# Another hand-written order of the steps in the two local-attention stages of a four-layer decoder trunk

## The chip, the core and the metric

The kernel runs on one core of one Trainium2 chip. Its time is that of one launch on the device in microseconds (us). Five engines with an instruction queue each share the work: TensorE (PE, matmuls and transposes; PEld are its weight loads), VectorE (DVE), ScalarE (ACT), GpSimd (POOL) and SyncE (SP, which here issues the loads of weights). An engine takes its instructions in the order in which they stand in its queue; between engines semaphores order the work.

## The reference, cut to what matters

A trunk of four layers over 256 rows of 1024 numbers in float32. Each layer has a token mixer, a cross-attention and a gated MLP, each followed by a LayerNorm. The mixers of layers 0 and 3 are the local attention that the change touches:

```
qkv = x @ w_qkv                                   # 16 query heads, 4 key/value groups, 64 wide
q, k = apply_rope(q), apply_rope(k)
scores = einsum('bnqhgd,bnkhd->bnhgqk', qb, kb) * 64 ** -0.5      # 128-row blocks, own and previous block
scores = where(valid, scores, -1e30)
probs = softmax(concatenate([scores, sink], -1))[..., :-1]        # a learned sink per head
out = einsum('bnhgqk,bnkhd->bnqhgd', probs, vb).reshape(...) @ w_o
```

## The kernel before, in words

Weights come from memory in pieces of up to 1 MB (`raw`). ACT casts each piece to a high part (`whi`, line 287) and DVE subtracts to get the low part (`wlo`, line 288), four pairs of 512 columns for a piece; a large product is then three matmuls (high by high, high by low, low by high). Four split pieces can be held; a slot comes free when the last matmul on its piece is done. A piece is split by ticks that the large matmuls give, so casts and subtractions stand between the other instructions of ACT and DVE.

A local-attention stage (function `swa`) first projects keys and values. Then `play` walks through a string of tokens, `SWA_SEQ`, a letter for the step and a number for the key group (0 to 3; a group has four query heads):

- Q: query projection of a group, 48 large matmuls (line 352) into one bank of PSUM.
- R: rotary on DVE, lines 685 to 689: three products from PSUM and a sum into `ropet`.
- K: keys to the layout with the head dimension on partitions: 8 transposes (line 359), two copies on ACT into `kT` (line 773).
- U: the same for the group's queries: 4 transposes, one copy on ACT into `qT` (line 699).
- S: scores: 8 small matmuls for the first row block and 8 for the second as the trace counts them, into four banks; DVE adds the mask and takes the maximum of each head (line 722, 8 instructions), three small ones (lines 725 to 727), and ACT takes 9 exponentials (lines 728 and 731).
- N: DVE sums, takes the reciprocal and multiplies (lines 737 to 740).
- T: 12 transposes of the probabilities into three banks, three copies on ACT into `pt` (line 750).
- P: probabilities by values, then a cast on ACT (`oh`, line 370) and a subtraction on DVE (`ol`, line 371).
- C: a chunk of the output projection, 12 matmuls of 512 columns. W loads the square-root table on ACT (line 408), G loads the LayerNorm's vectors.

The four tiles of the last two groups go through `op.finish`, where the LayerNorm begins. PSUM has eight banks, and from the first C on the output holds four of them.

```
def q_turn(g):
    ...
    A.copy(out=qT, in_=tp)
...
def scores(g):
    ...
    last[0] = A.activation(out=pr[:, hd], in_=pr[:, hd], func=AF.Exp, ...)
...
play(SWA_SEQ, {"Q": q_proj, "K": k_turn, "R": q_rope, "U": q_turn, "S": scores, "N": normalize, "T": turn, "P": pv, ...})
```

The tokens set in which order the steps are handed over. A scheduler then places each engine's instructions by its own estimate of when they are ready, so the queue of an engine can hold the steps in another order than the string; that order is fixed when the kernel is built. The two stages run from the same string, but what surrounds them differs, and so can their queues.

Of the kernel before, what the change touches and what calls it, by code (L numbers as in the profile page):

```python
# [32 lines left out]
PHASES = [("mem", 0)]  # L33
for _i in range(DEPTH):
    PHASES += [(("swa", "rglru", "mla")[_i % 3], _i), ("cross", _i), ("ffn", _i)]
SWA_SEQ = ("Q0 R0 Q1 R1 U0 Q3 K0 U1 R3 S0 S1 N0 Q2 T0 U3 P0 R2 U2 S3 N1 N3 T1 S2 C0 P1 N2 C1 W0 T2 T3 C2 P2 P3 "
           "C3 G0")
RG_SEQ = ("a2 t0 b2 V1 a3 V0 V2 b3 A1 V3 g0 h0 A2 g2 A0 g1 A3 R3 R2 R0 R1 h1 Z0 E0 g3 E1 h3 Y0 C0 G0 h2 E2 E3 "
          "C1 Y1 C2 Y2 Y3 W0 C3")
# [16 lines left out]
def _plan():  # L56
# [8 lines left out]
    def cols_piece(key, name, idx, cols):  # L65
        n = (cols.stop - cols.start) if isinstance(cols, slice) else len(cols)
        add(key, KC * n, lambda I: _b_piece(I[name] if idx is None else I[name][idx], cols))

    def halves(tag, name, idx, cols):
        n = (cols.stop - cols.start) if isinstance(cols, slice) else len(cols)  # L70
        for h in range(2):
            add((tag, h), 4 * n, lambda I, h=h: _b_piece(
                (I[name] if idx is None else I[name][idx])[512 * h:512 * h + 512], cols))

    def order(seq, pieces):
        for tok in seq.split():
            for toks, fn in pieces:
                if tok in toks.split():
                    pieces.remove((toks, fn))
                    fn()  # L80
                    break
# [7 lines left out]
    def outs(tag, name, idx):  # L89
        return [(f"C{2 * c} C{2 * c + 1}", lambda c=c: out_piece(tag, name, idx, c)) for c in range(2)]  # L90
# [5 lines left out]
    def piece_swa(i):  # L96
        j = i // 3
        halves(("kv", i), "a_w_qkv", j, slice(1024, 1536))
        order(SWA_SEQ, [(f"Q{g}", lambda g=g: cols_piece(("q", i, g), "a_w_qkv", j, slice(256 * g, 256 * g + 256)))
                        for g in range(A_G)] + outs(("mo", i), "a_w_o", j))  # L100
# [234 lines left out]
def trunk(ctx, tc, x_in, xT_in, memT_in, w, par, con, sinks, ln_g, ln_b, out):  # L335
# [70 lines left out]
    def want_sqrt(last):  # L406
        with tc.issue_after(ins_of(last)):
            A.activation(out=epsl[:, 2:3], in_=epsl[:, 0:1], func=AF.Sqrt)
# [202 lines left out]
    def play(seq, table):  # L611
        for tok in seq.split():
            table[tok[0]](int(tok[1]))
# [46 lines left out]
    def swa(mx, i, rest):  # L660
# [119 lines left out]
        def gb(_):  # L780
            norm[0] = Norm(op.y, mx, "p1", 2, i, 0)

        play(SWA_SEQ, {"Q": q_proj, "K": k_turn, "R": q_rope, "U": q_turn, "S": scores, "N": normalize, "T": turn, "P": pv,
                       "C": chunk, "G": gb, "W": lambda _: want_sqrt(last[0])})
# [493 lines left out]
```

## Time and profile before

| | us |
|---|---|
| median of 3 runs | 1384.0 (1383.43 to 1384.91) |
| the profiled execution | 1384.68 |
| its span, first to last instruction | 1382.7 |
| PE busy | 1363.8 (99%) |
| DVE busy | 1084.8 (78%) |
| ACT busy | 881.1 (64%) |
| first local attention, from its first query projection to the last C ahead of the finish | 65.7 to 119.85 |
| second local attention, end of the same stretch | 1113.56 |

A matmul's record runs until its results are out, so records overlap and PE looks busy through short waits. Waits are better seen at the weight loads (PEld): each load is followed by its matmul, and an idle time in front of a load is a wait. The granted clock of TensorE stands in the tables by stretch.

### The profile page before, as it was taken

To read this page: it belongs to the slowest core of one execution; us is meant where nothing else is said; L and a number is where in the kernel's file an instruction comes from. 1 tells how busy PE (TensorE), PEld (TensorE's weight loads), DVE (VectorE), ACT (ScalarE), POOL (GpSimd) and SP (SyncE) were. 2 spreads that over 40 slices of the span, in tenths; PEclk is the share of its full clock that TensorE was granted. 3 is DMA by queue.
4 is the path that set the end of the run, shared out by engine and by line. 5 is a ranking of instruction groups with operands and counts; after the bars stand their busy time and mean duration, and the time that the engine had idled before them with its cause. 6 is when DMAs were issued, how large, how long until landed. Compare 5 with 4: busy or idle time off the path is not lost.

```text
span 1382.7 us, 23749 instructions
## 1 busy us (share of the span) xinstructions
PE 1363.8 (99%) x9110; PEld 1232.0 (89%) x9110; DVE 1084.8 (78%) x2392; ACT 881.1 (64%) x1892; POOL 13.0 (1%) x28
## 2 busy tenths in 40 slices
PE   8999999999999999999999999999999999999997
PEld 8887989999898898999988898999998789899996
DVE  6887869777788878877778687977779867797775
ACT  6666747555579666655557664855565856675553
POOL 0000000000000000000000000000000000000000
PEclk9999999999999999999999999999999999999999
DMA  8733536555535554655526442555554326455550
GB/s 319 273 137 122 203 104 246 205 189 183 183 123 184 199 196 168 225 187 183 179 103 236 153 176 99 214 214 185 192 195 148 135 94 228 166 214 183 185 182 31
DMA packets 39393, 246.78 MB, mean 178 GB/s; under 512 B 4336, under 2 KB 6640, under 8 KB 12400
## 3 DMA queue, kind: packets, MB, share of 16 engines
q1 hardware_dynamic: 35824, 232.69, 46.3%
q0 software_dynamic: 3456, 12.58, 2.7%
q8 instruction: 71, 1.16, 0.3%
q14 instruction: 42, 0.34, 0.1%
HBM read 244.21 MB, written 1.05 MB: 177 GB/s over the span
## 4 chain that ended last, share of the span: by engine, by line
PE 92%; ACT 3%; DVE 3%; issue 0%; DMA 0%; SPq 0%; DVEq 0%; ACTq 0%
PE ps L352 89%; PE ps L359 3%; ACT p L731 2%; DVE p L722 1%; DVE wlo L288 1%; DMA raw<-in_w_dram 0%; DVE tt L834 0%; ACT whi L287 0%; DVE x L478 0%; DVE x L480 0%; DVE x L454 0%; DVE tt L832 0%; ACT oh L370 0%; ACT tt L861 0%; DVE ropet L689 0%
## 5 line engine op out<-in xcount | busy, mean ns | idle before, releaser
L288 DVE TENSOR_TENSOR wlo<-raw,whi 128x512 fp32r<-128x512 f32 (+1 forms) x869 | 559.1, 683 | 149.5 <-ACT whi L287 143.0
L287 ACT CAST whi<-raw 128x512 fp32r<-128x512 f32 (+1 forms) x869 | 485.9, 619 | 174.6 <-PE ps L352 150.2
L352 PE MATMUL ps<-xh,whi 128*128 128x256 f32 x1504 | 421.2, 280 | 0.0
L352 PE MATMUL ps<-xh,wlo 128*128 128x256 f32 x1504 | 420.1, 279 | 0.0
L352 PE MATMUL ps<-xl,whi 128*128 128x256 f32 x1504 | 419.8, 279 | 0.0
L352 PEld LDWEIGHTS ps<-xl,whi 128*128 128x128 f32 x1504 | 282.7, 188 | 1.9
L352 PEld LDWEIGHTS ps<-xh,whi 128*128 128x128 f32 x1504 | 282.7, 188 | 1.8
L352 PEld LDWEIGHTS ps<-xh,wlo 128*128 128x128 f32 x1504 | 282.6, 188 | 0.0
L1151 DVE SCALAR_TENSOR_TENSOR cv<-ps,part,cv 128x255 f32<-128x255 f32 (+1 forms) x352 | 166.3, 477 | 3.8 <-ACT cv L1149 1.4
L352 PE MATMUL ps<-whi,xh 128*128 128x512 f32 (+3 forms) x336 | 118.4, 353 | 0.4 <-ACT xh L370 0.2
L352 PE MATMUL ps<-wlo,gh 128*128 128x512 f32 x352 | 116.0, 396 | 0.0
L352 PE MATMUL ps<-whi,gh 128*128 128x512 f32 x352 | 115.9, 396 | 0.0
L352 PE MATMUL ps<-wlo,xh 128*128 128x512 f32 (+3 forms) x336 | 115.7, 345 | 0.0
L352 PE MATMUL ps<-whi,gl 128*128 128x512 f32 x352 | 115.1, 393 | 0.0
L1149 ACT ACTIVATE cv<-ps,part 128x256 f32<-128x256 f32 x176 | 98.3, 563 | 16.9 <-DVE cv L1151 5.5
L370 ACT CAST gh<-cv 128x256 fp32r<-128x256 f32 x88 | 35.7, 406 | 107.2 <-DVE cv L1166 107.0
L352 PE MATMUL ps<-whi,oh 128*128 128x512 f32 x256 | 92.9, 403 | 3.4 <-ACT oh L370 3.4
L352 PE MATMUL ps<-whi,xl 128*128 128x512 f32 (+3 forms) x336 | 92.6, 347 | 0.0
L352 PE MATMUL ps<-wlo,oh 128*128 128x512 f32 x256 | 90.8, 394 | 0.0
L352 PE MATMUL ps<-whi,ol 128*128 128x512 f32 x256 | 90.6, 395 | 0.0
L352 PEld LDWEIGHTS ps<-whi,gl 128*128 128x128 f32 x352 | 66.3, 188 | 15.8
L352 PEld LDWEIGHTS ps<-wlo,gh 128*128 128x128 f32 x352 | 66.4, 189 | 15.3
(227 smaller groups left out, 1842.1 us busy)
## 6 DMA issues: line engine op xcount, KB each, us to landing
raw<-in_w_dram SPq DMA_DIRECT2D x210, 1024.0 KB, 4.8
lng<-in_ln_g_dram POOLq DMA_DIRECT2D x12, 512.0 KB, 4.5
lnb<-in_ln_b_dram POOLq DMA_DIRECT2D x12, 512.0 KB, 6.2
raw<-in_w_dram SPq DMA_DIRECT2D x5, 768.0 KB, 4.7
raw<-in_w_dram SPq DMA_DIRECT2D x5, 256.0 KB, 6.1
raw<-in_w_dram SPq DMA_DIRECT2D x2, 640.0 KB, 3.7
xf<-in_xT_dram SPq DMA_DIRECT2D x1, 1024.0 KB, 8.6
x<-in_x_dram SPq DMA_DIRECT2D x1, 1024.0 KB, 13.2
```

The lines of the kernel that those rows point to most:

```text
L287: self.nc.scalar.copy(out=hi[:, c], in_=raw[:, c])
L288: self.nc.vector.tensor_tensor(out=lo[:, c], in0=raw[:, c], in1=hi[:, c].bitcast(F32), op=ALU.subtract)
L352: T.matmul(o, lhsT=l, rhs=r, start=st, stop=sp, **kw)
L359: T.transpose(o, i, ident)
L370: a = A.copy(out=hi, in_=src)
L722: V.tensor_tensor_reduce(out=pr[:, hd], in0=sc[e][:, c], in1=mk, scale=1.0, scalar=-3e38, op0=ALU.add, op1=ALU.max, accum_out=m[:, tb, hd: ...
L731: last[0] = A.activation(out=pr[:, hd], in_=pr[:, hd], func=AF.Exp, scale=A_D ** -0.5, bias=nm[:, b, hd:hd + 1], accum_out=sm[:, b, hd:hd ...
L1149: A.activation(out=dst, in_=src, func=AF.Identity, scale=wc[:, taps - 1:taps], bias=bias)
L1151: V.scalar_tensor_tensor(out=dst[:, d:], in0=src[:, :S - d], scalar=wc[:, taps - 1 - d:taps - d], in1=dst[:, d:], op0=ALU.mult, op1=ALU.add)
```

## The change

Only the string of tokens is changed. What each step computes is the same.

```
-SWA_SEQ = ("Q0 R0 Q1 R1 U0 Q3 K0 U1 R3 S0 S1 N0 Q2 T0 U3 P0 R2 U2 S3 N1 N3 T1 S2 C0 P1 N2 C1 W0 T2 T3 C2 P2 P3 "
-           "C3 G0")
+SWA_SEQ = ("Q0 R0 Q1 R1 K0 U0 U1 S0 S1 Q2 N0 R2 Q3 N1 R3 T0 U2 P0 T1 S2 P1 U3 S3 C0 N2 C1 W0 N3 C2 T2 T3 P2 P3 "
+           "C3 G0")
```

The keys' transposes and the scores of groups 0 and 1 now stand right behind Q0 and Q1, and the projections Q2 and Q3 follow them without a step between. Group 2 goes ahead of group 3 in everything that follows, U3 stands behind P1, and N3 behind C1. The pieces of weights for Q2 and Q3 change places with them.

ACT's queue of the first stage, before, from the copies of T0 on (p_1121 and p_1186 are the scores of groups 3 and 2):

```order
L750 COPY pt<-ps 128x512 x3
L699 COPY qT<-ps 128x512
L287 CAST whi<-raw 128x512 x2
L370 CAST oh<-ps 128x2x2x128
L699 COPY qT<-ps 128x512
L287 CAST whi<-raw 128x512 x2
L750 COPY pt<-ps 128x512 x3
L731 ACTIVATE p_1121,sm<-p_1121,nm 128x128
L728 ACTIVATE es<-es 128x8
L731 ACTIVATE p_1121,sm<-p_1121,nm 128x128 x3
L731 ACTIVATE p_1122,sm<-p_1122,nm 128x256 x4
```

The same place in the changed kernel, from the copies of T1 on (p_1137 and p_1138 are the scores of group 2, p_1193 and p_1194 those of group 3):

```order
L750 COPY pt<-ps 128x512 x3
L287 CAST whi<-raw 128x512
L370 CAST oh<-ps 128x2x2x128
L728 ACTIVATE es<-es 128x8
L731 ACTIVATE p_1137,sm<-p_1137,nm 128x128 x4
L731 ACTIVATE p_1138,sm<-p_1138,nm 128x256 x4
L699 COPY qT<-ps 128x512
L731 ACTIVATE p_1193,sm<-p_1193,nm 128x128
L728 ACTIVATE es<-es 128x8
L731 ACTIVATE p_1193,sm<-p_1193,nm 128x128 x3
L731 ACTIVATE p_1194,sm<-p_1194,nm 128x256 x4
L408 ACT_TABLE_LOAD
```

Before, both late copies into `qT` stand ahead of all exponentials of groups 3 and 2. In the changed kernel the copy for group 3 stands behind the nine exponentials of group 2.

The second stage of the changed kernel, the same place on ACT (p_12021 and p_12022 belong to group 2):

```order
L750 COPY pt<-ps 128x512 x3
L287 CAST whi<-raw 128x512
L370 CAST oh<-ps 128x2x2x128
L699 COPY qT<-ps 128x512
L731 ACTIVATE p_12021,sm<-p_12021,nm 128x128
L728 ACTIVATE es<-es 128x8
L731 ACTIVATE p_12021,sm<-p_12021,nm 128x128 x3
L731 ACTIVATE p_12022,sm<-p_12022,nm 128x256 x4
```

Here the copy for group 3 stands ahead of the exponentials of group 2.

PE's queue of the first stage in the changed kernel, behind Q3 (T0, U2, P0, T1, S2, P1, U3, S3, and the first row of C0):

```order
L359 MATMUL ps<-cont,p_863 128x128 x4
L359 MATMUL ps<-cont,p_864 128x128 x8
L359 MATMUL ps<-cont,ropet 128x128 x4
L352 MATMUL ps<-pt,va 64x256 x6
L359 MATMUL ps<-cont,p_901 128x128 x4
L359 MATMUL ps<-cont,p_902 128x128 x8
L352 MATMUL ps<-kT,qT 128x128 x4
L352 MATMUL ps<-kT,qT 128x256 x4
L352 MATMUL ps<-pt,va 64x256 x6
L359 MATMUL ps<-cont,ropet 128x128 x4
L352 MATMUL ps<-kT,qT 128x128 x4
L352 MATMUL ps<-kT,qT 128x256 x4
```

Between S2 (seventh and eighth row) and S3 (the last two) only P1 and U3 are left; before, S3 came first, then T1, and S2 behind it. The chunks C0, C1 and the first half of those that follow stand behind S3.

## Rows read from the trace of the kernel before

**Rows 1.** The page: busy time by engine, and the chain that ended last.

```profile
PE 1363.8 (99%) x9110; PEld 1232.0 (89%) x9110; DVE 1084.8 (78%) x2392; ACT 881.1 (64%) x1892; POOL 13.0 (1%) x28
...
PE 92%; ACT 3%; DVE 3%; issue 0%; DMA 0%; SPq 0%; DVEq 0%; ACTq 0%
```

**Rows 2.** The chain in order of time: start us, length us, what; projection Q3.

```profile
77.65 5.70 PE ps L352 x48
```

**Rows 3.** Weight loads, first stage: start, length, what, [idle before <- releaser].

```profile
84.57 2.53 PEld L352 LDWEIGHTS ps<-kT,qT 64*128 64x128 f32 x32 [0.17 <-ACT kT L773]
...
93.78 0.42 PEld L359 LDWEIGHTS ps<-cont,p 128*128 128x128 f32 x4 [0.61 <-issue]
94.92 0.86 PEld L359 LDWEIGHTS ps<-cont,p 128*128 128x128 f32 x8 [0.72 <-issue]
...
96.61 0.20 PEld L352 LDWEIGHTS ps<-pt,va 128*64 128x64 f32 x4 [0.40 <-ACT pt L750]
...
100.26 1.29 PEld L359 LDWEIGHTS ps<-cont,p 128*128 128x128 f32 x12 [0.33 <-issue]
101.72 1.18 PEld L352 LDWEIGHTS ps<-kT,qT 64*128 64x128 f32 x16 [0.17 <-issue]
103.23 0.30 PEld L352 LDWEIGHTS ps<-whi,oh 128*128 128x128 f32 x2 [0.33 <-DVE m L725]
...
117.11 2.36 PEld L352 LDWEIGHTS ps<-pt,va 128*64 128x64 f32 x24 [0.36 <-ACT pt L750]
119.85 0.30 PEld L352 LDWEIGHTS ps<-whi,oh 128*128 128x128 f32 x2 [0.39 <-issue]
...
122.48 0.19 PEld L352 LDWEIGHTS ps<-whi,oh 128*128 128x128 f32 x1
```

**Rows 4.** Instructions of DVE in order of time, first stage.

```profile
79.12 0.68 DVE L689 TENSOR_TENSOR ropet<-ropet,ropeu 128x512 f32<-128x512 f32 x1
...
83.37 0.69 DVE L685 TENSOR_TENSOR ropet<-ps,cont 128x512 f32<-128x512 f32 x1 [1.76 <-PE ps L352]
...
84.64 0.68 DVE L288 TENSOR_TENSOR wlo<-raw,whi 128x512 fp32r<-128x512 f32 x1
85.24 0.68 DVE L689 TENSOR_TENSOR ropet<-ropet,ropeu 128x512 f32<-128x512 f32 x1
85.84 0.28 DVE L722 CUSTOM_DVE_ANT_0 p<-ps,cont 128x128 f32<-128x128 f32 x1
...
92.55 0.16 DVE L737 TENSOR_TENSOR sm<-sm,es 128x8 f32<-128x8 f32 x1
...
94.72 0.68 DVE L685 TENSOR_TENSOR ropet<-ps,cont 128x512 f32<-128x512 f32 x1
```

**Rows 5.** Instructions of ACT in order of time, first stage.

```profile
78.30 1.66 ACT L287 CAST whi<-raw 128x512 fp32r<-128x512 f32 x3
...
92.39 0.19 ACT L728 ACTIVATE es<-es 128x8 f32<-128x8 f32 x1
...
95.99 1.53 ACT L750 COPY pt<-ps 128x512 f32<-128x512 f32 x3
...
99.41 0.60 ACT L699 COPY qT<-ps 128x512 f32<-128x512 f32 x1
...
111.39 1.28 ACT L408 ACT_TABLE_LOAD   x1
```

**Rows 6.** Weight loads of the second stage: first of the chunk ahead of the finish.

```profile
1113.56 0.30 PEld L352 LDWEIGHTS ps<-whi,oh 128*128 128x128 f32 x2 [0.39 <-issue]
```

**Rows 7.** Stretches at the launch's two ends: PE, PEld, DVE, ACT, POOL (count), clock, DMA.

```profile
8.40:13.20 4.80, 4.75 (x21) 4.52 (x22) 4.03 (x7) 3.72 (x7) 0.00 (x0) 1.00 1.04 397
13.40:20.00 6.60, 6.60 (x58) 6.60 (x58) 4.60 (x8) 3.67 (x7) 0.00 (x0) 1.00 0.81 305
...
1375.00:1376.00 1.00, 0.30 (x2) 0.00 (x0) 0.66 (x3) 0.69 (x2) 0.00 (x0) 1.00 0.66 250
...
1378.00:1380.00 2.00, 0.00 (x0) 0.00 (x0) 1.59 (x4) 0.00 (x0) 0.00 (x0) 0.65 0.09 34
```

## The prediction

> **What bounds the kernel now.** I read the page's busy times first, then the chain that ended last, then the two local-attention stages engine by engine. PE is busy 99% of the span and carries 92% of the chain [rows 1]. Its work is not changed, only its order, so the time can move only by waits of PE. Outside the two stages every queue reads as before. In each stage I therefore looked for the moment when chunk C3, the last piece of PE work ahead of the finish, can begin: 119.85 us in the first stage [rows 3], 1113.56 us in the second [rows 6]. Waits show in front of the weight loads. In the first stage the largest behind Q2 are 0.61, 0.72 and 0.40 us in front of T0's and P0's loads [rows 3], 1.73 us together. PE has run out of projections there and waits for probabilities and copies.
>
> **First stage, up to the scores of groups 0 and 1.** Before, U0 lies between Q1 and Q3; Q3 begins at 77.65 [rows 2], and 4 of the 12 transposes that T1 does in 1.46 us (100.26 to 101.72 [rows 3]) are 0.5, so Q1 ends near 77.15. K0 and U0 follow, 12 transposes, until 78.5. U1 needs the rotated queries of group 1, whose last instruction on DVE starts at 79.12 and takes 0.68 [rows 4]: PE waits some 1.4 us until 79.9. Before, Q3 lay over that. The copy of group 1's qT stands on ACT behind three casts of 1.66 us [rows 5]; with K0's and U0's copies in front they run from 79.3 to 80.95, and the copy ends at 81.55. A set of scores costs 1.5 us (101.72 to 103.23 [rows 3]), so S0 and S1 end at 83.1. DVE reaches the first reduction behind the last of those casts, at 81.7 instead of 85.84: 4.1 us earlier.
>
> **The cover.** Q2 and Q3 are 5.70 us each [rows 2] and now lie in one piece, 83.1 to 94.5. From the first reduction to the end of a group's exponentials it took 6.55 us (85.84 to 92.39), and the second group's took 3.6 more (to 95.99) [rows 4, 5]. Both sets therefore end at 88.25 and 91.85, under the projections. N0 costs 2.17 us (92.55 to 94.72 [rows 4]) and ends at 90.5. The 0.61 and 0.72 us of waits for T0's probabilities go. That is the gain of the change.
>
> **What is late next.** DVE has no pause from N0 on. R2 up to its last sum costs 1.27 us (83.37 to 84.64 [rows 4]), to 91.8; the first subtraction waits for ACT's cast behind the exponentials (92.45), and with it, the sum, one more subtraction (0.60 us each, 84.64 to 85.24) and N1's two products the queue is at 96.1. Then a subtraction, R3 with one inside (1.27 + 0.6 + 0.6), three subtractions and the subtraction for group 0's output, 0.6 each: 96.1 + 0.6 + 2.47 + 1.8 + 0.6 = 101.6. Only there does S2's first reduction start, though PE does S2 from about 99.3 to 100.8 (from 94.5 on: T0 1.46, U2 0.5, P0 1.4, since two P take 117.11 to 119.85 [rows 3], T1 1.46, S2 1.5). With the 6.55 us from there to the end of the exponentials and one subtraction put between the reductions (0.6), ACT is done with group 2 at 108.75. The copy of group 3's qT stands behind these exponentials and takes 0.60 [rows 5]: 109.35. PE has finished P1 and U3 (1.4 and 0.5) at 102.7, and its next instruction is S3, which needs that copy. Behind S3 stand three chunks that are ready, but PE takes its matmuls in order. **PE waits some 6.7 us.**
>
> From 109.4: S3 1.5 us, three times 12 matmuls of a chunk at 2.63 (119.85 to 122.48 [rows 3]), to 118.8; T2, to 120.25. T3 needs banks that T2's copies free. On ACT those come late: N2 on DVE holds S3's reductions until 110.9, the exponentials end 6.55 later at 117.45, the table load takes 1.28 [rows 5], four casts 2.1 (three took 1.66), and each copy 0.5 (three took 1.53 [rows 5]). The second copy ends at 121.95, T3 at 122.45, P2 and P3 take 2.8, and C3 begins at 125.25 instead of 119.85: **5.4 us later**, at full clock.
>
> The wait also costs clock. [...] What that costs shows at the start: in 8.4 to 13.2, among PE's first matmuls, 4.80 us held 21 matmuls, while 6.60 us of 13.4 to 20.0 held 58, so 21 should take 2.4 [rows 7]. (The clock column reads 1.00 there; the spacing tells more.) One return costs about 2.4 us, of which I take 2.2, since part of S3 is bound by its weight loads. Of it 0.8 falls into T3's wait for banks (without that wait T3 would end at 121.7 instead of 122.45), and C3 begins 1.4 us later still, near 126.65: **6.8 us**.
>
> [...]
>
> **Second stage.** C3 stood 993.7 us behind that of the first stage (1113.56 less 119.85 [rows 3, 6]), so I move the sums by some 993.5. U1 waits as above. S2's first reduction comes at 1095.0, its exponentials end 7.15 us later at 1102.15. Here the copy of qT stands ahead of them, so S3 waits only for that copy (about 1 us behind U3), and S3's reductions stand ahead of N2, so its exponentials follow at once, 3.6 us, to 1105.75. Table load, four casts and three copies bring T3's last group to 1110.9, P2 and P3 to 1113.7, and C3 begins near 1113.75: **+0.2 us**. The waits that go and those that come cancel. From both sides: without the casts in front of the copies PE would set the end, 1.7 us earlier; were S3 held as in the first stage, it would be 5.4 later, with a copy ahead of the exponentials at most 1.5.
>
> **Sum.** 6.8 + 0.2 = 7.0 us on the profiled execution's 1384.68 gives 1391.7. That execution is 0.7 above the median of the three runs, 1384.0, so the number for the median is **1391.0**. SP's and POOL's queues keep their order, and a later stage only gives the weights' transfers more time, so I cost them at nothing; were a transfer late, one piece would be some 5 us late, which I hold for unlikely.
>
> **Rivals.** The wait without the clock: the level falls too late, or what it costs lies in T3's wait. 5.4 + 0.2 gives 1389.6. For it speaks that waits up to 0.7 us [rows 3] left no trace in the clock; against it, that 6.7 us is of another size.
>
> A longer return: at the launch's start slow matmuls came ahead of 8.4 us too. If S3 and the chunks behind it lose twice the 2.2 us, 1393.2.
>
> ACT gets to the copy in time. If the first stage ran as the second does, with the copy ahead of the exponentials and S3's reductions ahead of N2, it would end like it, +0.2 each: no change, 1384.4. The order of ACT's queue speaks against it. [...]
>
> Faster: PE is the bound from Q3 on. The remaining work (four T at 1.46, four P at 1.4, two U at 0.5, two S at 1.5, three chunks at 2.63: 23.3 us) would bring C3 to 117.8, 2.05 us earlier, and the second stage about as much: 4.1 us less, 1379.9. It decides itself at S3: group 3's copy must end by 102.7, when U3 does, and T2's copies must come ahead of the casts. With a free DVE S2's reductions would start at 99.5 instead of 101.6, and the first stage would still wait over 4 us at S3.
>
> **How the numbers follow.** The forecast 0.56, the wait without the clock 0.20, the longer return 0.12, no wait 0.07, faster 0.05. My chain of DVE sums can be off by 1.5 us either way, so the range goes from 1388.5 (the case without the clock, and 1.1 less) to 1393.6 (the longer return, and 0.4 more); the last two cases and tails are left out, about 0.2. A measurement of this kernel can tell 0.2%, 2.8 us, from no change: slower by more than that has the first three cases, 0.88; within it 0.07; faster 0.05.
>
> **What would show it.** Right: in the first stage a gap of 5 to 8 us in front of S3's weight loads with ACT's copy into qT as its releaser, none in the second; a granted clock under 1 inside or behind that gap, and S3 and C0 at wide spacing; gaps of 1.5 and 1.8 us ahead of U1; hardly any between Q3 and S2; C3 near 126.7 in the first stage, and the second stage as long as before. Wrong: S3 follows U3 at once in the first stage, the clock stays at 1.00 through the gap, or the second stage has a wait of its own of over 2 us.

## The result, and the profile after

| | before | after |
|---|---|---|
| median of 5 runs, us | 1384.46 (1383.43 to 1384.91) | 1393.41 (1392.16 to 1393.51) |
| the profiled execution, us | 1384.68 | 1392.82 |
| its span, us | 1382.7 | 1390.6 |
| mean granted clock | 0.999 | 0.996 |

The ratio of after to before is 1.0061, with a 95% interval of 1.0050 to 1.0073: slower by 0.6%, 2.4 us above the forecast and inside its range.

The page gives the same total of busy time on PE as [rows 1], but PE's share of the chain is 90% instead of 92%, and DVE has 5% instead of 3%:

```profile
PE 1363.7 (98%) x9110; PEld 1233.9 (89%) x9110; DVE 1085.1 (78%) x2392; ACT 881.0 (63%) x1892; POOL 13.0 (1%) x28
...
PE 90%; DVE 5%; ACT 3%; issue 1%; DMA 1%; SPq 0%; DVEq 0%; ACTq 0%
```

Weight loads of the first stage after, the answer to [rows 3] (start, length, what, [idle before <- releaser]):

```profile
79.70 0.42 PEld L359 LDWEIGHTS ps<-cont,ropet 128*128 128x128 f32 x4 [1.57 <-DVE ropet L689]
...
94.47 1.33 PEld L359 LDWEIGHTS ps<-cont,p 128*128 128x128 f32 x12
...
102.27 0.42 PEld L359 LDWEIGHTS ps<-cont,ropet 128*128 128x128 f32 x4 [0.39 <-issue]
109.12 2.21 PEld L352 LDWEIGHTS ps<-kT,qT 64*128 64x128 f32 x16 [6.43 <-ACT qT L699]
111.98 0.38 PEld L352 LDWEIGHTS ps<-whi,oh 128*128 128x128 f32 x2 [0.65 <-DVE m L722]
...
120.13 2.77 PEld L359 LDWEIGHTS ps<-cont,p 128*128 128x128 f32 x24
123.07 2.36 PEld L352 LDWEIGHTS ps<-pt,va 128*64 128x64 f32 x24 [0.17 <-issue]
125.81 0.30 PEld L352 LDWEIGHTS ps<-whi,oh 128*128 128x128 f32 x2 [0.38 <-issue]
```

The pauses of [rows 3] in front of T0's loads are gone. Behind U3 (102.27) PE stands still for 6.43 us, and S3 takes 2.86 us (109.12 to 111.98), where a set of scores took 1.51 in [rows 3] (101.72 to 103.23). C3 begins at 125.81 instead of 119.85.

ACT in that place, against [rows 5]: the copy into `qT` starts at 108.50, behind the exponentials of group 2, which begin at 104.89.

```profile
104.89 0.21 ACT L728 ACTIVATE es<-es 128x8 f32<-128x8 f32 x1 [1.92 <-DVE es L727]
...
108.50 0.56 ACT L699 COPY qT<-ps 128x512 f32<-128x512 f32 x1
...
117.79 1.28 ACT L408 ACT_TABLE_LOAD   x1
```

DVE, against [rows 4]: the first rotation of keys, an instruction that both kernels have ahead of everything changed (it starts at 60.70 before), and S2's first reduction, which sets when those exponentials can begin:

```profile
60.55 0.42 DVE L619 TENSOR_TENSOR ropet<-ps,cont 128x256 f32<-128x256 f32 x1 [0.48 <-ACT va L667]
...
101.48 0.28 DVE L722 CUSTOM_DVE_ANT_0 p<-ps,cont 128x128 f32<-128x128 f32 x1
```

The stretches around the gap (the column behind the busy times is the granted clock): PE's weight loads stop at 102.7, the clock falls between 105 and 106 (0.68 on average), reads 0.50 from 106 to 112, so also while S3 runs, and 0.91 in 112 to 113.

```profile
104.00:105.00 1.00, 0.00 (x0) 0.00 (x0) 0.93 (x8) 0.11 (x1) 0.00 (x0) 1.00 0.87 213
105.00:106.00 1.00, 0.00 (x0) 0.00 (x0) 0.46 (x1) 1.00 (x6) 0.00 (x0) 0.68 0.97 410
106.00:109.00 3.00, 0.00 (x0) 0.00 (x0) 0.33 (x2) 3.00 (x13) 0.00 (x0) 0.50 0.34 139
109.00:112.00 3.00, 2.88 (x17) 2.06 (x17) 2.71 (x11) 0.07 (x1) 0.00 (x0) 0.50 0.00 0
112.00:113.00 1.00, 1.00 (x6) 0.87 (x5) 0.92 (x5) 0.00 (x0) 0.00 (x0) 0.91 0.00 0
```

The second stage, against [rows 6]: S3 waits 0.97 us there, and T3 waits for banks that ACT's copies free.

```profile
1104.69 1.18 PEld L352 LDWEIGHTS ps<-kT,qT 64*128 64x128 f32 x16 [0.97 <-ACT qT L699]
...
1117.65 0.91 PEld L359 LDWEIGHTS ps<-cont,p 128*128 128x128 f32 x8 [1.44 <-ACT pt L750]
...
1121.46 0.30 PEld L352 LDWEIGHTS ps<-whi,oh 128*128 128x128 f32 x2 [0.39 <-issue]
```

C3 stands 7.90 us behind that of [rows 6], more than the two stages give. The rest is lost in the mixer of layer 2 (MLA), whose instructions stand in the same order in both kernels. PE's waits in 690 to 830 us, after (line, releaser: sum, times, longest); before, the same line has 0.6:

```profile
PEld ps L352 <- ACT cqh L922: 1.8, 1, 1.8
```

ACT's cast ahead of that one waits for a weight transfer:

```profile
739.12 0.62 ACT L287 CAST whi<-raw 128x512 fp32r<-128x512 f32 x1 [1.09 <-DMA raw<-in_w_dram]
```

So that each part can be compared over all kernels, I cut every trace at the same instructions: the first rotation of keys, the first load of C3 in the first stage, a run of seven casts that ACT has in the MLA stage ahead of the late transfer, a load of the LayerNorm's transposed rows at the head of layer 3 (1052.99 before), and C3 of the second stage. The table gives what each distance adds to the kernel before, in us, by the profiled execution. "Timed" is the difference of the medians of one comparison. In the last two rows the cut at C3 is taken at the first of the added matmuls, which stand just ahead of C3, so they count in the second column. The sum leaves out what lies ahead of the first cut, which differs by 1.8 us over these profiles and that of the kernel before (the first rotation starts between 59.73 and 61.54). The profiled execution of the kernel changed in the first stage only was the longest of its five (1393.53, median 1391.7).

```
                                  1st stage  to MLA     MLA    2nd stage  to the end   sum   timed
changed kernel                      +6.11      0.0     +1.27     +0.68        0.0      +8.1   +8.95
 again, first                       +6.50      0.0     +1.06     +0.70       -0.1      +8.2
 again, second                      +7.08      0.0     +0.71     +0.67        0.0      +8.5
changed in the first stage only     +7.34      0.0     +1.27      0.0        -0.1      +8.6   +7.0
changed in the second only           0.0       0.0     +0.1      +0.69        0.0      +0.7   +0.7
changed, PE kept busy in the gap    +5.58     -0.1     +0.1      +0.70        0.0      +6.3   +6.2
U3 ahead of S2                      +0.48      0.0     +0.1      -0.26        0.0      +0.3   +0.4
 and the table load late            -1.08     +0.4     +0.1      -1.75        0.0      -2.4   -3.2
 and the casts late                 -1.72     +2.1     +0.8      -1.78       +2.1      +1.5   +0.7
changed, table load late            +7.25      0.0      0.0      -0.79        0.0      +6.5   +6.85
before, 28 matmuls more              0.0      +6.4      0.0       0.0         0.0      +6.4   +5.4
before, 33 matmuls more              0.0      +7.5      0.0       0.0         0.0      +7.5   +7.7
```

### The profile page after: what moved, and what is told of

It is laid out like the page before. It is cut to its first block, busy times and chain, and to the rows that moved or that the text cites. A ratio compares the mean times of both kernels' runs of the same rounds, so it can differ in the third digit from the quotient of the medians.

```text
span 1390.6 us, 23757 instructions
## 1 busy us (share of the span) xinstructions
PE 1363.7 (98%) x9110; PEld 1233.9 (89%) x9110; DVE 1085.1 (78%) x2392; ACT 881.0 (63%) x1892; POOL 13.0 (1%) x28
## 3 DMA queue, kind: packets, MB, share of 16 engines
q8 instruction: 71, 1.16, 0.3%
## 4 chain that ended last, share of the span: by engine, by line
PE 90%; DVE 5%; ACT 3%; issue 1%; DMA 1%; SPq 0%; DVEq 0%; ACTq 0%
PE ps L352 87%; PE ps L359 3%; DVE wlo L288 2%; ACT p L731 1%; DMA raw<-in_w_dram 1%; ACT whi L287 1%; DVE p L722 0%; DVE tt L834 0%; DVE x L478 0%; DVE p L740 0%; DVE ropet L689 0%; ACT xh L370 0%; DVE x L480 0%; DVE ropeu L687 0%; DVE x L454 0%
```

## The experiments

My theory: the loss of the first stage is PE's wait for the copy into `qT`, by that copy's place in ACT's queue, with a price in clock beside it. The main rivals: the order of the projections itself costs the time, or the slow S3 has another cause. Behind each ratio its 95% interval stands in brackets.

**The copy ahead of the exponentials.**

```
-... T0 U2 P0 T1 S2 P1 U3 S3 C0 N2 C1 W0 N3 C2 T2 T3 P2 P3 C3 G0
+... T0 U2 P0 T1 U3 S2 P1 S3 C0 N2 C1 W0 N3 C2 T2 T3 P2 P3 C3 G0
```

> The changed order, but with U3 (group 3's transposes and the copy into qT) put ahead of S2 and P1 in both stages, so that ACT's copy stands ahead of group 2's exponentials. Theory (the wait comes from the place of that copy in ACT's queue): the 6.43 us ahead of S3 go, the clock stays at 1.00, S3's loads start near 103, and DVE's first reduction of S2 stays near 101.5, so the exponentials of both groups end near 111.7, table load, four casts and the copies follow, and C3 begins near 119.8 as in the kernel before; second stage +0 to +0.7: 1384 to 1385.5 us in all. Rival 1 (the order of the projections itself, with its pauses ahead of U1 and its late reductions, costs the time, and the gap only shows it): the wait moves to T2 or T3, C3 near 125, time 1391 or more. Rival 2 (PE becomes the bound from Q3 on): C3 near 117.8, time near 1380.

1385.1 us, ratio to before 1.0004 (0.9996 to 1.0013): as expected. The copy for group 3 now stands ahead of group 2's exponentials on ACT:

```profile
100.13 0.66 ACT L699 COPY qT<-ps 128x512 f32<-128x512 f32 x1
...
104.87 0.21 ACT L728 ACTIVATE es<-es 128x8 f32<-128x8 f32 x1 [1.43 <-DVE es L727]
```

Its weight loads, first stage:

```profile
102.73 1.18 PEld L352 LDWEIGHTS ps<-kT,qT 64*128 64x128 f32 x16 [0.38 <-issue]
104.24 0.30 PEld L352 LDWEIGHTS ps<-whi,oh 128*128 128x128 f32 x2 [0.33 <-DVE m L722]
...
116.32 0.91 PEld L359 LDWEIGHTS ps<-cont,p 128*128 128x128 f32 x8 [2.10 <-ACT pt L750]
```

S3 follows at 102.73, 6.4 us earlier, and lasts 1.51 us again. One token moved past two others gives back the loss but for 0.48 us of this stage, so the order of the projections does not cost it. Nor is PE the bound: a new wait of 2.10 us stands in front of T3. On ACT, in the same kernel, the copies that free T3's banks stand behind a table load and four casts:

```profile
112.23 1.28 ACT L408 ACT_TABLE_LOAD   x1
113.52 0.20 ACT L408 ACTIVATE epsl<-epsl 128x1 f32<-128x1 f32 x1
113.63 2.16 ACT L287 CAST whi<-raw 128x512 fp32r<-128x512 f32 x4
115.70 3.01 ACT L750 COPY pt<-ps 128x512 f32<-128x512 f32 x6
```

**One stage at a time.** Layer 0 and layer 3 get strings of their own, one the string before, the other the changed one.

```
-        play(SWA_SEQ, {...
+        play(SWA_SEQ3 if i else SWA_SEQ, {...
```

> The changed order in the first local-attention stage alone; the second keeps the order before. Theory: C3 of the first stage 5.96 us late as in the changed kernel, nothing more in the second: 1390.4 us; if the late weight transfer that cost the changed kernel another 1.2 us between the two stages comes with every shift of 6 us, 1391.7. Rival (the second stage is what costs, or the two add up otherwise): below 1389 or above 1393.

> The changed order in the second local-attention stage alone; the first keeps the order before. Theory: no wait ahead of S3, but T3 waits for banks behind the table load and four casts, C3 of that stage 0.7 us late: 1385.2 us, no difference that can be measured. The stage between them keeps its transfer in time, as nothing ahead of it is shifted. Rival (the changed order costs some 6 us wherever it stands): 1390.

The first stage alone: 1391.7 us, ratio 1.0055 (1.0042 to 1.0067). The second alone: 1385.45 us, ratio 1.0009 (1.0000 to 1.0018). The first carries the loss, the second 0.7 us. The first-only profile also shows that the clock's price is not the same each time. Its stretches: the clock fell later, in 106 to 109 (0.88 on average), and was still at 0.50 in 112 to 115, when PE did the first chunk:

```profile
106.00:109.00 3.00, 0.00 (x0) 0.00 (x0) 0.08 (x1) 3.00 (x15) 0.00 (x0) 0.88 0.40 167
109.00:112.00 3.00, 2.59 (x16) 2.04 (x16) 2.93 (x12) 0.35 (x1) 0.00 (x0) 0.50 0.00 0
112.00:115.00 3.00, 3.00 (x9) 2.15 (x8) 1.89 (x13) 0.67 (x4) 0.00 (x0) 0.50 0.00 0
115.00:118.00 3.00, 3.00 (x14) 2.51 (x13) 0.00 (x0) 3.00 (x14) 0.00 (x0) 0.98 0.01 3
```

Here C0 too runs slowly (3.95 us, against 2.71 in the changed kernel's profile), and the stage loses 7.34 us instead of 6.11, with the same instructions and the same gap of 6.43 us.

**The wait without the clock.**

```
-... S2 P1 U3 S3 C0 ...
+... S2 P1 U3 D0 S3 C0 ...
+        def keep(_):
+            if i == 0:
+                ps = bank()
+                for _ in range(24):
+                    mm(ps, mvh[:, 0, 0:P], mvh[:, 0, 0:512], True, True)
```

> The changed kernel, with 24 more matmuls of 512 columns (their result is used by nothing) between U3 and S3 of the first stage, so that PE has work in the gap. At 0.22 us each they take 5.3 of the 6.43 us. Theory (the wait costs clock beside itself): the granted clock stays at 1.00, S3 still starts at 109.1 but takes 1.5 us instead of 2.86, and C3 begins near 124.4 instead of 125.81: 1.4 us less than the changed kernel, 1392.0 us. Rival (S3 is slow for another reason, the slow reductions or the weight loads): S3 takes 2.86 us again, and the time is 1393.4. If the added matmuls run over the gap, S3 starts later than 109.1, and the time is longer by that.

1390.89 us, ratio to before 1.0047 (1.0033 to 1.0060). Its stretches and weight loads:

```profile
104.00:109.00 5.00, 4.25 (x21) 3.21 (x20) 1.68 (x9) 4.18 (x18) 0.00 (x0) 1.00 0.47 195
109.00:113.00 4.00, 4.00 (x27) 3.19 (x28) 3.97 (x19) 0.00 (x0) 0.00 (x0) 1.00 0.00 0
```

```profile
102.41 5.30 PEld L352 LDWEIGHTS ps<-mvh 128*128 128x128 f32 x24
108.89 1.18 PEld L352 LDWEIGHTS ps<-kT,qT 64*128 64x128 f32 x16 [1.17 <-ACT qT L699]
110.40 0.30 PEld L352 LDWEIGHTS ps<-whi,oh 128*128 128x128 f32 x2 [0.33 <-issue]
...
121.22 0.91 PEld L359 LDWEIGHTS ps<-cont,p 128*128 128x128 f32 x8 [0.85 <-ACT pt L750]
...
125.04 0.30 PEld L352 LDWEIGHTS ps<-whi,oh 128*128 128x128 f32 x2 [0.39 <-issue]
```

The clock stays at 1.00, S3 starts in the same place and lasts 1.51 us: work that nobody needs makes the stage shorter. C0 comes 1.34 us earlier against the first rotation, but C3 only 0.53: 0.85 falls into T3's wait for banks, which the changed kernel doesn't have because its PE is late by then. The mechanism is as expected, the stage's gain against the changed kernel's profile smaller than the 1.4 us I gave it. The timed difference (2.5 us between two comparisons, the intervals of whose ratios overlap) also holds the MLA's late transfer, absent in this profile.

**Does the late start alone make the transfer late?** In the string before, D0 as above, with 28 or 33 matmuls:

```
-... C2 P2 P3 C3 G0
+... C2 P2 P3 D0 C3 G0
```

> The kernel before, its order untouched, with 28 more matmuls of 512 columns (result used by nothing) between P3 and C3 of the first stage: no wait, no change of clock, everything behind 28 x 0.22 = 6.2 us later. It asks about the weight transfer of the MLA stage that landed late and cost 1.2 us in the two profiles that stood 6.1 and 7.3 us late, and not in the one that stood 5.6 late. Theory (the late start is enough): the wait ahead of the query transposes' copies grows from 0.6 to 1.8 us again, 1384.7 + 6.2 + 1.2 = 1392.1 us. Rival (it belongs to the changed order or to the clock): the wait stays 0.6, 1390.9 us.

> The same with 33 matmuls: 33 x 0.22 = 7.3 us later. Theory (the late start is enough): 1384.7 + 7.3 + 1.2 = 1393.2 us and a wait of 1.8 us in the MLA stage. Rival: 1392.0 us and 0.6.

1390.46 us (ratio 1.0041, 1.0027 to 1.0055) and 1392.74 us (1.0055, 1.0042 to 1.0068), and both profiles show the wait of before (line 928 is line 922 of the kernel before, as six lines were added):

```profile
PEld ps L352 <- ACT cqh L928: 0.6, 1, 0.6
```

The theory falls: 6.4 and 7.5 us of plain delay leave the transfer in time, in one profile each.

**The changed kernel again, and the term of the second stage.**

> The changed kernel, unaltered, profiled once more. It asks how much of its time differs from one execution to the next: the loss by the clock in the first stage, 0.5 us net in one profile and 1.8 in that of the kernel with the same first stage alone, and the MLA stage's wait for a late weight transfer, 1.8 us in both and 0.6 in every kernel without the cold stretch. Theory (both vary by chance): the wait in the MLA stage is 0.6 us in this profile or in the next, and the first stage differs by half a us or more between profiles. Rival (both belong to this program): a wait of 1.8 us in both profiles.

> The same kernel once more, for the same question: by the theory at least one of the two profiles shows a wait of 0.6 us in the MLA stage; by the rival both show 1.8.

(Without a cold stretch, that is without the fall of the clock in the first stage, it is not 0.6 in every kernel, as I wrote: with the casts late, below, it is 1.3.) The waits in the MLA stage are 1.6 and 1.3 us, neither 0.6 nor 1.8, and the first stage differs by 0.6 (+6.50 and +7.08): inconclusive for the transfer. But the price of the cold stretch does differ from one execution of the same program to the next: S3 takes 2.86 us in both, as in the first profile, and C0 behind it 3.11 and 3.66, where the first had 2.71.

```
-... C1 W0 N3 C2 T2 T3 P2 P3 C3 G0
+... C1 N3 C2 T2 T3 P2 P3 W0 C3 G0
-                A.copy(out=pt[:, t], in_=tp)
+                last[0] = A.copy(out=pt[:, t], in_=tp)
```

> The changed order, U3 left where the change put it, and only the table load for the square root put behind the copies of groups 2 and 3, in both stages. Theory (in the second stage T3 waits 1.44 us behind table load and casts, in the first PE is the bound again from S3 on): second stage 1.2 us shorter, that is 0.5 shorter than before instead of 0.7 longer; first stage unchanged at +6.1 (or 0.8 less, where T3 waits for banks): 1391.8 us beside the changed kernel's 1393.0 or so. Rival (the second stage's 0.7 us come from elsewhere): no change against the changed kernel.

1391.2 us, ratio to before 1.0046 (1.0032 to 1.0059). Second stage of this kernel:

```profile
1114.55 2.77 PEld L359 LDWEIGHTS ps<-cont,p 128*128 128x128 f32 x24
1117.49 2.36 PEld L352 LDWEIGHTS ps<-pt,va 128*64 128x64 f32 x24 [0.17 <-ACT pt L750]
```

T3's wait of 1.44 us is gone, and the stage is 1.47 us shorter than in the changed kernel: the table load in front of the copies was its loss. The MLA's wait is 0.6 us here although the cold stretch is there (S3 takes 2.87 us, and the launch's mean clock is 0.996 as in the changed kernel), so the cold stretch alone does not make the transfer late either.

**A version that beats both.** U3 ahead of S2, and the table load late:

```
-... T0 U2 P0 T1 S2 P1 U3 S3 C0 N2 C1 W0 N3 C2 T2 T3 P2 P3 C3 G0
+... T0 U2 P0 T1 U3 S2 P1 S3 C0 N2 C1 N3 C2 T2 T3 P2 P3 W0 C3 G0
-                A.copy(out=pt[:, t], in_=tp)
+                last[0] = A.copy(out=pt[:, t], in_=tp)
```

> The changed order with U3 ahead of S2 and P1, and the table load for the square root behind the six copies of probabilities of groups 2 and 3 instead of ahead of them, in both stages. Theory (T3 waits for banks because its copies stand behind a table load of 1.28 us and four casts of 2.16): T3's wait of 2.10 us in the first stage falls to 0.8, C3 begins 0.8 us earlier than in the kernel before, and in the second stage 1.5 earlier: 1382.4 us. Rival (group 3's probabilities or the finish, which now waits for the table, set the end): no gain, 1385.1 us.

1381.86 us, ratio to before 0.9978 (0.9970 to 0.9987): the fastest kernel of this study. T3's wait in the first stage has fallen from 2.10 to 0.60 us:

```profile
114.12 0.90 PEld L359 LDWEIGHTS ps<-cont,p 128*128 128x128 f32 x8 [0.60 <-ACT pt L750]
```

**The casts late too.**

```
+            if g == 3:
+                W.after = [ins_of(last[0])]
...
         def chunk(ci):
+            W.hold = ci < 3
```

> As the one before, and the four casts of weights are also put behind the copies, in both stages. Theory: T3 then waits only for group 3's probabilities, some 0.9 us; C3 begins about 1.5 us earlier than in the kernel before in the first stage and 2 in the second: 1381.3 us. Rival (the casts are late for the chunks and the finish that need them, or for the transfers that their buffers free): the wait moves into the finish, 1385 us or more.

1385.79 us, ratio 1.0007 (0.9998 to 1.0016): the rival. T3 no longer waits, and C3 comes 1.72 and 1.78 us earlier than before, but both finishes are 2.1 us longer. In the chain of work that ended last the casts' subtractions now stand between the steps of the LayerNorm, where the kernel before has PE throughout:

```profile
133.22 0.69 DVE xl L371
133.91 0.06 DVE mv L457
133.98 0.60 DVE wlo L288
134.57 0.60 DVE xl L371
```

## Why the prediction was right, point by point

- **Up to the scores and the cover: right.** S2's first reduction was put at 101.6 and came at 101.48; T0's loads, put at 94.5, start at 94.47 without a wait.
- **The wait in front of S3: right in place, cause and size.** Put at 6.7 us up to 109.4, it is 6.43 up to 109.12, released by the copy into `qT`. That the copy's place causes it is shown by moving U3: the wait goes, and with it all but 0.5 us of the loss.
- **The stage at full clock: 5.4 us forecast, 5.58 measured** with PE kept busy. The 0.8 us that T3's wait for banks should absorb is the 0.85 us of that profile.
- **The clock: right in kind, and its size is a spread and not a number.** I summed 2.2 us less 0.8, that is 1.4 net. That a wait of this size lowers the clock was my estimate; the changed kernel's profile shows it, 0.50 from 106 to 112. The 2.2 us came from slow matmuls at the launch's start, where the clock column reads 1.00, and no run shows that a lower clock slows those. What the runs showed in their place: S3 1.35 us longer, and C0 2.71 to 3.95 us long, where with PE kept busy it took 2.63. The five profiles with the cold stretch (mean clock 0.996, in the other eight 0.998 or 0.999) give 6.11, 6.50, 7.08, 7.25 and 7.34 less 5.58: 0.5 to 1.8, with a mean of 1.3. The rival without the clock is what the kernel with the busy PE does; it is not what the changed kernel does. Nor is it the longer return, though that rival's 1393.2 us lies nearer to the measured 1393.41 than the forecast does: it needed 3.6 us net, no profile shows more than 1.8, and its number is met by other terms.
- **The second stage: +0.2 forecast, +0.68 measured**, alone and in the changed kernel. The mis-sized term is the end of the exponentials: I put the table load behind them at 1105.75, and it starts at 1113.55, less the 7.22 us by which the whole stage is late 1106.33. Group 3's exponentials did not follow at once (lines below). The step behind it, copies behind table load and casts, is shown by the kernel with the late table load.
- **A term that the sum did not have: the MLA's weight transfer**, 1.27 us in this profile. I had costed later transfers at nothing, on the ground that a later stage only gives them more time. It is late in all three profiles of the changed kernel, in the one with the first stage alone, and with the casts late (1.3 us); it is in time with a plain delay of the same size, and in a kernel with the same cold stretch. Over all kernels it is late in four of five profiles with the cold stretch and in one of eight without. What decides it stays open: neither the delay nor the cold stretch is enough by itself, and with one profile for most kernels chance is not excluded.
- **The number.** The median is 2.4 us above the forecast: about 1.0 is the MLA's transfer (the mean of three profiles), 0.5 the second stage, and 0.5 the median of before, 1384.46 in this comparison and 1384.0 in the runs I started from. The first stage is 0.2 below the forecast in the mean of the three profiles (6.56 against 6.8). That leaves 0.6, and which of the varying terms makes it up (the time ahead of the first rotation is one) is not shown.

In the second stage of the changed kernel DVE has S3's reductions ahead of N2, as the prediction says, but the first step of N2 (line 737), which waits for the end of group 2's exponentials, stands ahead of S3's last two small instructions (lines 726 and 727):

```profile
1109.47 0.17 DVE L737 TENSOR_TENSOR sm<-sm,es 128x8 f32<-128x8 f32 x1 [1.36 <-ACT p L731]
...
1109.63 0.16 DVE L727 TENSOR_TENSOR es<-sinkt,m 128x8 f32<-128x8 f32 x1
```

So ACT waits 0.37 us between the two groups, most of the 0.58 by which the table load is late:

```profile
1109.82 0.40 ACT L731 ACTIVATE p<-p,nm 128x128 f32<-128x128 f32 x1 [0.37 <-DVE es L727]
```

One reading of the prediction is wrong, though its sum does not use it. The largest wait behind Q2 in the first stage of the kernel before is not 0.72 us but 1.16, in front of C2, whose input ACT casts only behind the exponentials of groups 3 and 2. The kernel before thus already paid for a short instruction behind another group's exponentials, and in the changed kernel this wait is gone:

```profile
111.42 0.30 PEld L352 LDWEIGHTS ps<-whi,oh 128*128 128x128 f32 x2 [1.16 <-ACT oh L370]
```

The rival in which PE is the bound from Q3 on fell with the first experiment: even with the copy early, C3 comes 0.48 us later than before, since ACT has a table load and casts in front of T2's copies. With the table load moved as well, 2.4 us of the 4.1 us that I gave that rival are there by the profile.

## What to carry to other kernels

When steps are reordered, read the queue of each engine that hands work back: a short copy behind another group's exponentials can cost more than the pauses that the new order removes, and moving one token past two others gave back nearly the whole loss. The wait of 6.43 us on TensorE was priced twice here, for itself and for the slow matmuls behind it, and the second price differed from profile to profile (0.5 to 1.8 us). Work that is needed late (a table load) should stand behind the copies that free banks, which made the second stage 1.47 us shorter here, but what is needed soon (the next casts) should not be pushed behind them: here each finish then took 2.1 us more.

## What the runs showed of the hardware that I had not expected

The same instructions up to the first chunk, with the same gap of 6.43 us, lost different amounts behind the gap in five profiles. S3 ran slowly in all five, 2.86 or 2.87 us instead of 1.51; the difference lies in the first chunk behind it, which took 2.71, 3.11, 3.66, 3.85 and 3.95 us, in the order of the losses. In the changed kernel's profile, the first of these, the clock was back at 0.91 in 112 to 113; in the profile with the first stage alone, the last of them (112.27 to 116.22), it was at 0.50 still in 112 to 115. For the three between them the mean clock of the launch is known, 0.996 as in those two. The timed runs don't show this spread by themselves: the kernel with the first stage alone spread over 2.4 us (1391.12 to 1393.53), but the kernel before, which has no such gap, over 2.5 in one comparison (1383.51 to 1386.04).
